# Encoder block, stage 1: V in 2 KB runs, stores issued by GpSimd, modulation sums spread over three projections

## The chip, the cores and the metric

The kernel runs on one core of one Trainium2 chip. The metric is the device time of one execution in microseconds (us), taken as the median of several runs.

## The reference

One encoder block over 1024 tokens of width 1024, all in float32, cut here to what stage 1 and its neighbours compute:

```python
mod = silu(c) @ w_ada + b_ada                 # six vectors of 1024
shift1, scale1, gate1, shift2, scale2, gate2 = split(mod, 6)
h = rms_norm(x, norm1_g) * (1 + scale1) + shift1
z = h @ w_in                                  # columns: c_q 256, c_kv 256, k_pe 64, dq 512, dk 512, dv 512
q  = rms_norm(c_q)  @ w_q_up                  # 4 heads x (128 + 64 rotary)
kv = rms_norm(c_kv) @ w_kv_up                 # 4 heads x (128 K + 128 V)
mla = softmax(q k^T) v                        # 4 heads
diff = (softmax(q1 k1^T) - lam * softmax(q2 k2^T)) dv   # 4 heads
x = x + gate1 * (concat[mla, diff] @ w_out)
h2 = rms_norm(x, norm2_g) * (1 + scale2) + shift2
x = x + gate2 * hier_moe(h2)                  # 32 experts
out = rms_norm(x, final_norm_g)
```

## The kernel before, in words

The kernel goes through stage 1 (all projections, to about 345 us of the span), the attention stage, the output projection with the router, and the experts. Every product in float32 precision is made of three passes (`mm3`, lines 67 to 69), from a high and a low part of each operand.

Stage 1 keeps the transposed, normalised activations (`hThi`, `hTlo`) in SBUF and walks over blocks of columns of `w_in`, and in each over 8 tiles of 128 tokens. A tile takes 24 matmuls (8 pieces of the width times three passes) into one PSUM buffer `pz` of four; DVE and ACT empty it. The blocks that matter here:

- The part called s1b makes dk. After four tiles come eight "flips": TensorE transposes four rotated tiles into a PSUM buffer `ptr` of two (line 180), ACT copies it to `stg` (line 409), DVE writes the low part `kl` (line 410), and both are stored to DRAM in `qk_d`. `stg` and `kl` share six buffers. The sixteen flips are woven into the following matmuls.
- The part s1c makes dv: `split_v` writes high and low part to `vs`, two buffers of one tile each, and stores each of the two with a DMA of 128 x 4 pieces of 512 bytes to `vd_d`.
- The part s1d makes c_q (g = 0) and c_kv with k_pe (g = 1). For each tile ACT sums the squares (line 472, output `junk`), ACT and DVE make the scale, DVE writes `cn`, and TensorE flips `cn`.
- The part s1e makes the MLA queries, keys and V from the latents: `split_v` again (to `vm_d`), and for heads 1 to 3 tiles `stg`, stored to `mq_d` by the helper `store`.

Beside this run the last four vectors of `mod` (gate1, shift2, scale2, gate2), which later stages read. `ada_in` loads 32 pieces `aw` of 512 KB of `w_ada`, three ahead; `ada_add` multiplies each by a column of silu(c) and adds it to `acc` (the first of eight on POOL, line 383, seven on DVE, line 385); the tables `AS` and `AC` say how many products belong to each tile of s1b and s1c. `ada_out` sums over the partitions with TensorE into a column of 128 x 8, adds the bias, and stores this column to `ada_d`, where the neighbours in memory lie on neighbouring partitions.

All loads and stores of stage 1 are issued by SP, in one order, each waiting for its data or its buffer. The order on the other engines is made by the scheduler of the kernel language from the program and its pools; what a pool's memory held before must be free before a new tile uses it. The attention stage begins with POOL scaling the exponentials `e` (lines 833, 776, 779), which TensorE then transposes.

```python
    def store(dst, src):
        Y.dma_start(f32(dst), f32(src))
...
                acc[v] = ap.tile([128, D], F32, name="acc", tag="acc")
                G.tensor_scalar(acc[v], w, sc[:, 0:1], 1.0, op0=ALU.mult, op1=ALU.mult)
...
        Y.dma_start(ada_d[0, (2 + v) * D:(3 + v) * D].rearrange("(j p) -> p j", p=128), col)
```

Of the kernel before, what the change touches and what calls it, by code (L numbers as in the profile page):

```python
# [9 lines left out]
F32 = mybir.dt.float32  # L10
F32R = mybir.dt.float32r
BF16 = mybir.dt.bfloat16
I32 = mybir.dt.int32
AF = mybir.ActivationFunctionType
ALU = mybir.AluOpType
# [5 lines left out]
D = 1024  # L21
# [10 lines left out]
LH = (3, 0)  # L32
XL = (0, 0, 0, 4)
WM = ((0, 1), (0, 1), (0, 0), (0, 0))
AS = (2, 2, 2, 2, 2, 2, 2, 2)
AC = (2, 2, 2, 2, 2, 2, 2, 2)
PF = 7
KJ, PL = 4, 6
GU1 = 10
# [10 lines left out]
def tile_hymba(  # L50
# [6 lines left out]
    V, A, G, T, Y = nc.vector, nc.scalar, nc.gpsimd, nc.tensor, nc.sync  # L57
    dbg = dbg or {}

    def f32(ap):  # L60
        return ap.bitcast(F32)
# [12 lines left out]
    ident = consts.tile([128, 128], F32, name="ident")  # L74
# [14 lines left out]
    ada_d = dram.tile([1, 6 * D], F32, name="ada_d")  # L89
# [27 lines left out]
    hTlo = hTp.tile([128, 8, S], F32R, name="hTlo")  # L117

    def store(dst, src):
        Y.dma_start(f32(dst), f32(src))  # L120

    def w_tiles():
        return (wp.tile([128, 4, 512], F32, name="wraw", tag="wraw", bufs=2),
# [62 lines left out]
        V.scalar_tensor_tensor(lo, src_lo, scale, f32(hi_lo), op0=ALU.mult, op1=ALU.subtract)  # L186

    def split_v(pool, pz, dst, t):
        vs = pool.tile([128, 2, 512], F32R, name="vs", tag="vs", bufs=2)
        A.copy(vs[:, 0], pz)  # L190
        V.tensor_sub(vs[:, 1], pz, f32(vs[:, 0]))
        for l in range(2):
            Y.dma_start(f32(dst[:, :, t, l].rearrange("h p d -> p h d")),
                        f32(vs[:, l].rearrange("p (h d) -> p h d", h=4)))

    def zps():
        return ps1.tile([128, 512], F32, name="pz", tag="z", bufs=4)
# [149 lines left out]


    aps = ExitStack()
    ap = aps.enter_context(tc.tile_pool(name="s1m", bufs=2, side="right", **RT))  # L350

    aw, acc = {}, {}

# [6 lines left out]
    def ada_out(v):  # L360

        pr = mps()
        for j in range(8):
            T.matmul(pr[:, j:j + 1], acc[v][:, j * 128:(j + 1) * 128], ones[:, 0:1], start=True, stop=True)
        col = ap.tile([128, 8], F32, name="col", tag="col")
        V.tensor_add(col, pr[:, 0:8], colsb[:, 16 + 8 * v:24 + 8 * v])
        Y.dma_start(ada_d[0, (2 + v) * D:(3 + v) * D].rearrange("(j p) -> p j", p=128), col)

    def ada_add(n):

        for _ in range(n):
            i = ada_at[0]
            ada_at[0] += 1
            if i == 0:
                for k in range(AB):
                    ada_in(k)
            v, k = divmod(i, 8)
            if k == KO and v:
                ada_out(v - 1)
            w = aw.pop(i)  # L380
            if k == 0:
                acc[v] = ap.tile([128, D], F32, name="acc", tag="acc")
                G.tensor_scalar(acc[v], w, sc[:, 0:1], 1.0, op0=ALU.mult, op1=ALU.mult)
            else:
                V.scalar_tensor_tensor(acc[v], w, sc[:, k:k + 1], acc[v], op0=ALU.mult, op1=ALU.add)
            ada_in(i + AB)
# [45 lines left out]
    with tc.tile_pool(name="s1c", bufs=2, **RT) as sb:  # L432
        w = in_w(1600, 512)
        for t in range(NT):
            if t == 4:
                in_w(0, 256)
            pz = zps()
            in_proj(t, 512, w, pz)
            split_v(sb, pz, vd_d, t)
            ada_add(AC[t])  # L440
        ada_out(3)
    aps.close()

    cTp = cTs.enter_context(tc.tile_pool(name="cT", bufs=1, side="right", **RT))
    cThi = cTp.tile([128, 4, S], F32R, name="cThi")
# [8 lines left out]
    with tc.tile_pool(name="s1d", bufs=2, **RT) as sb:  # L454
        for g in range(2):
            width = 320 if g else 256
            w = in_w(256 * g, width)
            for half in range(2):
                if half:
                    if g:  # L460
                        up_w = [load_up(w_q_up, 768), load_up(w_kv_up, 1024)]
                    else:
                        in_w(256, 320)
                cns, rps = [], []
                hs = slice(half * 512, half * 512 + 512)
                for t in range(4 * half, 4 * half + 4):
                    pz = zps()
                    in_proj(t, width, w, pz[:, :width])
                    cn = sb.tile([128, 256], F32, name="cn", tag="cn", bufs=6)
                    junk = sb.tile([128, 256], F32, name="junk2", tag="junk2", bufs=1)  # L470
                    st = sb.tile([128, 4], F32, name="st2", tag="st2", bufs=4)
                    A.activation(junk, pz[:, :256], AF.Square, accum_out=st[:, 0:1])
                    A.activation(st[:, 1:2], st[:, 0:1], AF.Sqrt, bias=epsc, scale=1.0 / 256)
                    V.reciprocal(st[:, 2:3], st[:, 1:2])
                    V.tensor_scalar(cn, pz[:, :256], st[:, 2:3], None, op0=ALU.mult)
                    cns.append(cn)
                    if g:
                        rp = sb.tile([128, 1, 2, 64], F32, name="rpk", tag="rpk", bufs=5)
                        rope(sb, pz[:, 256:320].rearrange("p (m h d) -> p m h d", m=1, h=2), 1, t, rp)
                        rps.append(rp)  # L480
                for j in range(2):
                    jj = 2 * g + j
                    ptr = flip([cn[:, j * 128:j * 128 + 128] for cn in cns])
                    gcol = colsb[:, 56 + jj:57 + jj]
                    A.activation(cThi[:, jj, hs], ptr, AF.Copy, scale=gcol)
                    V.scalar_tensor_tensor(cTlo[:, jj, hs], ptr, gcol, f32(cThi[:, jj, hs]),
                                           op0=ALU.mult, op1=ALU.subtract)
                if g:
                    ptr = flip([rp[:, 0].rearrange("p c d -> p (c d)") for rp in rps])
                    A.copy(K1pe[:, hs], ptr)  # L490
                    V.tensor_sub(KLpe[:, hs], ptr, f32(K1pe[:, hs]))
    qw, kw = up_w
    hTs.close()

# [28 lines left out]
    with tc.tile_pool(name="s1e", bufs=2, **RT) as sb:  # L523
        load_head("d", 0, 0)
        load_head("d", 0, 1)
        heads["m", 0] = [[tile_a() for _ in range(5)], None]

        def to_m(h, i, hs):

            if h == 0:  # L530
                return heads["m", 0][0][i][:, hs], lambda: None
            st = sb.tile([128, 512], F32R, name="stg", tag="stg", bufs=6)
            return st, lambda: store(mq_d[h, i, :, hs], st)

        qv = [w_.rearrange("p r (h e) -> p r h e", h=4)[:, :, :, 128:192] for w_ in qw]
        kv = [w_.rearrange("p r (h e) -> p r h e", h=4)[:, :, :, 128:256] for w_ in kw]
        for half in range(2):
            hs = slice(half * 512, half * 512 + 512)
            rps = []
            for t in range(4 * half, 4 * half + 4):  # L540
                ts = slice(t * 128, t * 128 + 128)
                pz = zps()
                for r in range(2):
                    mm3(pz[:, :256], cThi[:, r, ts], cTlo[:, r, ts], qv[0][:, r], qv[1][:, r], r == 0, r == 1)
                rp = sb.tile([128, 4, 2, 64], F32, name="rpq", tag="rpq", bufs=6)
                rope(sb, pz[:, :256].rearrange("p (m h d) -> p m h d", m=4, h=2), 4, t, rp)
                rps.append(rp)
                pz = zps()
                for r in range(2):
                    mm3(pz, cThi[:, 2 + r, ts], cTlo[:, 2 + r, ts], kv[0][:, r], kv[1][:, r], r == 0, r == 1)  # L550
                split_v(sb, pz, vm_d, t)
            for h in range(4):
                ptr = flip([rp[:, h].rearrange("p c d -> p (c d)") for rp in rps])
                st, put = to_m(h, 4, hs)
                split_q(st, st[64:128], ptr, ptr[64:128], st[64:128], MSC)
                put()
        for h in range(4):
            for src, (whi, wlo), base in ((0, qw, h * 192), (2, kw, h * 256)):
                for half in range(2):
                    hs = slice(half * 512, half * 512 + 512)  # L560
                    pz = zps()
                    for r in range(2):
                        mm3(pz, whi[:, r, base:base + 128], wlo[:, r, base:base + 128],
                            cThi[:, src + r, hs], cTlo[:, src + r, hs], r == 0, r == 1)
                    (sh, put_h), (sl, put_l) = to_m(h, src, hs), to_m(h, src + 1, hs)
                    if src == 0:
                        split_q(sh, sl, pz, pz, sh, MSC)
                    else:
                        A.copy(sh, pz)
                        V.tensor_sub(sl, pz, f32(sh))  # L570
                    put_h()
                    put_l()
# [981 lines left out]
```

## Time and profile before

| | |
|---|---|
| median of 3 runs | 1444.3 us (1442.43 to 1444.31) |
| the profiled execution, whole time | 1447.06 us |
| its span, first to last instruction | 1445.3 us |
| TensorE matmul busy | 1337.1 us (93%) |
| VectorE (DVE) busy | 993.9 us (69%) |
| ScalarE (ACT) busy | 681.8 us (47%) |
| GpSimd (POOL) busy | 416.9 us (29%) |
| moved by DMA | 361.22 MB, mean 250 GB/s |

Busy times are of one execution, and an engine's share is over the whole span. PE is TensorE's matmuls, PEld its weight loads; SPq is SP's queue of DMAs. "Idle before <- X" is the time an engine stood still before an instruction, and what ended it. The granted clock is the share of full speed that TensorE was given: 1.0 is its level of 2.4 GHz and 0.5 its level of 1.2 GHz, and a stretch with something between had both. The DMA share is the mean busy share of the 16 DMA engines.

### The profile page before, as it was taken

The page shows a single profiled execution, that of the slowest core. Times are in us where ns is not written, and L with a number is a line of the kernel's source. Part 1 is how long each engine was busy: PE and PEld are TensorE (multiplying, and loading weights), DVE is VectorE, ACT ScalarE, POOL GpSimd, SP SyncE. Part 2 cuts the span into 40 slices and gives each one's busy share as a digit, 9 for nine tenths or more (in the row PEclk, how much of TensorE's full clock was granted, in tenths as well). Part 3 has the DMA queues.
Part 4 walks back from the last instruction along what each step waited for, and adds up shares of the span by engine and source line. Part 5 has one row for each costly group of instructions (what it writes and reads, how often), then busy time and mean ns, then how long its engine had stood idle before and what let it go on. Part 6 is the DMA issues. An engine that isn't in the chain of part 4 may idle for free. (4 is left out here: it accounts for less than half of the span.)

```text
span 1445.3 us, 17733 instructions
## 1 busy us (share of the span) xinstructions
PE 1337.1 (93%) x6211; PEld 961.9 (67%) x6211; DVE 993.9 (69%) x1530; ACT 681.8 (47%) x1058; POOL 416.9 (29%) x285
## 2 busy tenths in 40 slices
PE   5799896998999999989995999999999998999993
PEld 4578676986788888878884655566565555656541
DVE  6888553475788888884568766676766668666646
ACT  4642212454766666661214554444554444544523
POOL 3100000002766666650002233333333322111231
PEclk9899898999999999999995999999999999999995
DMA  9537799268043433337968999999988998999956
GB/s 328 150 100 249 198 298 209 55 223 302 1 152 125 139 130 140 132 112 261 340 224 297 339 354 315 348 366 354 345 297 297 327 348 308 347 359 338 372 181 238
DMA packets 197502, 361.22 MB, mean 250 GB/s; under 512 B 20101, under 2 KB 62146, under 8 KB 195874
## 3 DMA queue, kind: packets, MB, share of 16 engines
q1 hardware_dynamic: 132946, 228.97, 47.2%
q10 hardware_dynamic: 57024, 113.25, 21.9%
q0 software_dynamic: 7440, 17.84, 5.2%
q8 instruction: 50, 0.82, 0.2%
q14 instruction: 42, 0.34, 0.1%
HBM read 306.52 MB, written 61.88 MB: 255 GB/s over the span
## 5 line engine op out<-in xcount | busy, mean ns | idle before, releaser
L1153 DVE TENSOR_TENSOR ra<-rb,ra 128x1024 fp32r<-128x1024 f32 x180 | 210.8, 1217 | 42.4 <-ACT ra L1152 42.2
L1152 ACT CAST ra<-rb 128x1024 fp32r<-128x1024 f32 x180 | 181.5, 1050 | 93.4 <-PE pg L69 34.2
L1319 POOL DMA_INDIRECT x_d<-y,tg x32 | 139.2, 4351 | 132.5 <-DVE y L1351 130.3
L1349 PE MATMUL pd<-rb,hmT 128*96 128x512 f32 x368 | 165.1, 592 | 0.0
L604 PE MATMUL s<-ra 128*128 128x512 f32 x448 | 129.5, 405 | 2.5 <-ACT e L625 2.4
L1351 DVE SCALAR_TENSOR_TENSOR y<-pd,wt,ra 96x512 f32<-96x512 f32 x64 | 47.8, 747 | 121.5 <-PE pd L1349 121.5
L67 PE MATMUL pz<-whi,hThi 128*128 128x512 f32 (+2 forms) x320 | 122.3, 382 | 9.6 <-ACT hThi L255 5.1
L625 ACT ACTIVATE e<-s,mx 128x1024 f32<-128x1024 f32 x96 | 107.6, 1120 | 38.5 <-DVE mx L620 21.8
L620 DVE TENSOR_REDUCE mx<-s 128x1 f32<-128x1024 f32 x96 | 116.6, 1217 | 12.2 <-PE s L604 12.2
L68 PE MATMUL pz<-wlo,hThi 128*128 128x512 f32 (+2 forms) x320 | 120.6, 377 | 1.5 <-DVE wlo L131 1.5
L930 POOL DMA_INDIRECT xb<-h_d,tg x31 | 31.5, 1017 | 313.4 <-PE ptr L1326 312.8
L69 PE MATMUL pz<-whi,hTlo 128*128 128x512 f32 (+2 forms) x320 | 116.0, 370 | 0.3 <-DVE hTlo L257 0.3
L67 PE MATMUL pg<-ra,xT 128*96 128x512 f32 x256 | 114.1, 446 | 0.2 <-ACT xT L1369 0.2
L1349 PEld LDWEIGHTS pd<-rb,hmT 128*96 128x96 f32 x368 | 58.2, 163 | 77.6 <-issue 74.5
L68 PE MATMUL pu<-ra,xT 128*96 128x512 f32 x256 | 102.6, 401 | 3.7 <-DVE ra L1153 3.7
L69 PE MATMUL pg<-ra,xT 128*96 128x512 f32 x256 | 102.1, 399 | 2.8 <-DVE xT L1370 2.8
L67 PE MATMUL pu<-ra,xT 128*96 128x512 f32 x256 | 103.7, 405 | 0.0
L1153 DVE TENSOR_TENSOR ra<-rx,ra 128x1024 fp32r<-128x1024 f32 x76 | 89.6, 1217 | 19.2 <-ACT ra L1152 19.2
L636 ACT CAST rb<-ptr 128x512 fp32r<-128x512 f32 x128 | 74.4, 588 | 59.8 <-PE ptr L632 59.2
L68 PE MATMUL pg<-ra,xT 128*96 128x512 f32 x256 | 102.0, 398 | 0.0
L69 PE MATMUL pu<-ra,xT 128*96 128x512 f32 x256 | 100.7, 393 | 0.0
L1152 ACT CAST ra<-rx 128x1024 fp32r<-128x1024 f32 x76 | 76.8, 1047 | 38.6 <-PE pg L69 11.5
(336 smaller groups left out, 2813.2 us busy)
## 6 DMA issues: line engine op xcount, KB each, us to landing
rb<-in_w_expert_up_dram ACTq DMA_DIRECT2D x26, 1024.0 KB, 16.7
rb<-in_w_expert_down_dram ACTq DMA_DIRECT2D x26, 1024.0 KB, 9.2
rb<-in_w_expert_gate_dram ACTq DMA_DIRECT2D x24, 1024.0 KB, 12.7
rb<-in_w_expert_gate_dram SPq DMA_DIRECT2D x20, 1024.0 KB, 15.6
rb<-in_w_expert_down_dram SPq DMA_DIRECT2D x20, 1024.0 KB, 9.2
rb<-in_w_expert_up_dram SPq DMA_DIRECT2D x19, 1024.0 KB, 10.3
aw<-in_w_ada_dram SPq DMA_DIRECT2D x32, 512.0 KB, 5.0
ra<-qk_d SPq DMA_DIRECT2D x24, 512.0 KB, 6.0
```

Source lines behind the costliest of these rows:

```text
L67: T.matmul(ps, ahi, bhi, start=first, stop=False)
L68: T.matmul(ps, ahi, blo, start=False, stop=False)
L69: T.matmul(ps, alo, bhi, start=False, stop=last)
L604: T.matmul(ps[:, ns], l, r[:, ns], start=i == 0, stop=i == len(parts) - 1)
L620: V.reduce_max(mx, ps, axis=AX.X, negate=True)
L625: A.activation(e, ps, AF.Exp, bias=nb, scale=1.0, accum_out=z)
L636: A.copy(hi[:, :, q], src)
L1152: A.copy(hi, raw[:, 2 * half:2 * half + 2])
L1153: V.tensor_sub(lo, raw[:, 2 * half:2 * half + 2], f32(hi))
L1319: G.indirect_dma_start(out=x2_d, out_offset=bass.IndirectOffsetOnAxis(ap=si, axis=0), in_=y, in_offset=None, bounds_check=S - 1, oob_is_er ...
L1349: T.matmul(pd, hT[:, k], w[:, k], start=k == 0, stop=k == 3)
L1351: V.scalar_tensor_tensor(y[:, ns], pd, wcol, gate2[:, ns], op0=ALU.mult, op1=ALU.mult)
```

## The change

- `store` issues on POOL's queue in place of SP's; this takes in the stores of `qk_d`, `mq_d` and both V.
- `split_v` gathers two token tiles in a `vs` of twice the size and stores them with one DMA of 128 x 4 pieces of 2 KB, in place of four DMAs of 128 x 4 pieces of 512 bytes.
- The modulation products go one to a tile (`AS`, `AC`, and a new `AG` for s1d) in place of two; their pool moves to the left side of SBUF and closes after s1d.
- The first product of each vector is made by ACT in place of POOL.
- `ada_out` transposes its column to 8 rows of 128, ACT copies them, and POOL's queue stores 8 runs of 512 bytes.
- In s1e `stg` and `rpq` have five buffers in place of six.

```diff
-AS = (2, 2, 2, 2, 2, 2, 2, 2)
-AC = (2, 2, 2, 2, 2, 2, 2, 2)
+AS = (1, 1, 1, 1, 1, 1, 1, 1)
+AC = (1, 1, 1, 1, 1, 1, 1, 1)
+AG = ((1, 1, 1, 1, 1, 1, 1, 1), (1, 1, 1, 1, 1, 1, 1, 1))
     def store(dst, src):
-        Y.dma_start(f32(dst), f32(src))
+        G.dma_start(f32(dst), f32(src))
     def split_v(pool, pz, dst, t):
-        vs = pool.tile([128, 2, 512], F32R, name="vs", tag="vs", bufs=2)
-        A.copy(vs[:, 0], pz)
-        V.tensor_sub(vs[:, 1], pz, f32(vs[:, 0]))
-        for l in range(2):
-            Y.dma_start(f32(dst[:, :, t, l].rearrange("h p d -> p h d")),
-                        f32(vs[:, l].rearrange("p (h d) -> p h d", h=4)))
+        if t % 2 == 0:
+            vpair.append(pool.tile([128, 4, 2, 2, 128], F32R, name="vs", tag="vs", bufs=2))
+        hi, lo = (vpair[-1][:, :, t % 2, l] for l in range(2))
+        pv4 = pz.rearrange("p (h d) -> p h d", h=4)
+        A.copy(hi, pv4)
+        V.tensor_sub(lo, pv4, f32(hi))
+        if t % 2:
+            store(dst[:, :, t - 1:t + 1].rearrange("h p t l d -> p h (t l d)"),
+                  vpair[-1].rearrange("p h t l d -> p h (t l d)"))
-    ap = aps.enter_context(tc.tile_pool(name="s1m", bufs=2, side="right", **RT))
+    ap = aps.enter_context(tc.tile_pool(name="s1m", bufs=2, **RT))
-        Y.dma_start(ada_d[0, (2 + v) * D:(3 + v) * D].rearrange("(j p) -> p j", p=128), col)
+        T.transpose(pr[0:8, 128:256], col, ident)
+        row8 = ap.tile([8, 128], F32, name="row8", tag="row8")
+        A.copy(row8, pr[0:8, 128:256])
+        G.dma_start(ada_d[0, (2 + v) * D:(3 + v) * D].rearrange("(j p) -> j p", p=128), row8)
-                G.tensor_scalar(acc[v], w, sc[:, 0:1], 1.0, op0=ALU.mult, op1=ALU.mult)
+                A.activation(acc[v], w, AF.Copy, scale=sc[:, 0:1])
...
+                    ada_add(AG[g][t])
+                if g == 1 and half:
+                    ada_out(3)
-            st = sb.tile([128, 512], F32R, name="stg", tag="stg", bufs=6)
+            st = sb.tile([128, 512], F32R, name="stg", tag="stg", bufs=5)
-                rp = sb.tile([128, 4, 2, 64], F32, name="rpq", tag="rpq", bufs=6)
+                rp = sb.tile([128, 4, 2, 64], F32, name="rpq", tag="rpq", bufs=5)
```

The order of SP's queue from the end of s1c into s1d, before (`wraw` are pieces of `w_in` and of the two up-projections):

```order
L358 DMA aw<-in_w_ada_dram 128x1024 x2
L193 DMA vd_d<-vs 128x4x128 x2
L358 DMA aw<-in_w_ada_dram 128x1024
L367 DMA ada_d<-col 128x8x1
L193 DMA vd_d<-vs 128x4x128 x2
L129 DMA wraw<-in_w_in_dram 128x4x320
L367 DMA ada_d<-col 128x8x1
L129 DMA wraw<-in_w_in_dram 128x4x320
L449 DMA wraw<-in_w_q_up_dram 128x2x768
L449 DMA wraw<-in_w_kv_up_dram 128x2x1024
```

And SP's whole queue from s1b to the end of s1d in the change (line 358 of before is 365 here, 129 is 131, 449 is 457):

```order
L131 DMA wraw<-in_w_in_dram 128x4x256
L365 DMA aw<-in_w_ada_dram 128x1024 x13
L131 DMA wraw<-in_w_in_dram 128x4x256
L365 DMA aw<-in_w_ada_dram 128x1024 x2
L131 DMA wraw<-in_w_in_dram 128x4x320
L365 DMA aw<-in_w_ada_dram 128x1024 x10
L131 DMA wraw<-in_w_in_dram 128x4x320
L365 DMA aw<-in_w_ada_dram 128x1024 x2
L457 DMA wraw<-in_w_q_up_dram 128x2x768
L365 DMA aw<-in_w_ada_dram 128x1024 x4
L457 DMA wraw<-in_w_kv_up_dram 128x2x1024
```

The stores have left SP's queue, and four `aw` loads now stand ahead of the keys' up-projection.

POOL's order around the end of stage 1, before:

```order
L383 TENSOR_SCALAR acc<-aw,sc 128x1024 x4
L833 TENSOR_SCALAR e<-e,zd 128x1024
L776 TENSOR_SCALAR e<-e,zd 128x1024
L779 TENSOR_TENSOR e<-e 128x512 x2
```

And in the change, from the V of s1c on (lines 833 and 776 of before are 845 and 788):

```order
L122 DMA vd_d<-vs 128x4x512 x3
L377 DMA ada_d<-row_1634 8x128
L122 DMA vd_d<-vs 128x4x512
L377 DMA ada_d<-row_1957 8x128
L122 DMA vm_d<-vs 128x4x512 x2
L122 DMA mq_d<-stg 128x512 x3
L122 DMA vm_d<-vs 128x4x512 x2
L122 DMA mq_d<-stg 128x512 x27
L845 TENSOR_SCALAR e<-e,zd 128x1024
L788 TENSOR_SCALAR e<-e,zd 128x1024
```

Twenty-seven stores in a row stand on POOL ahead of its first instruction of the attention stage.

## Rows read from the trace of the kernel before

**Rows 1.** Busy time by stretch, s1b to s1e; the first line names the columns.

```profile
core 0: us, PE busy (x) PEld busy (x) DVE busy (x) ACT busy (x) POOL busy (x), PEclk, DMA share, GB/s
138.00:345.00 207.00, 184.64 (x1025) 160.22 (x1023) 115.50 (x214) 68.68 (x144) 3.37 (x3) 0.93 0.76 211
```

**Rows 2.** Timeline of PE, 138 to 262 us: instructions after a long idle time.

```profile
148.89 0.65 PE L180 MATMUL ptr<-ident,rp 128*128 128x128 f32 x4 [2.03 <-DVE kl L410]
...
178.44 1.11 PE L180 MATMUL ptr<-ident,rp 128*128 128x128 f32 x4 [4.91 <-DVE kl L410]
...
183.29 1.11 PE L180 MATMUL ptr<-ident,rp 128*128 128x128 f32 x4 [1.18 <-DVE kl L410]
...
229.18 0.58 PE L67 MATMUL pz<-whi,hThi 128*128 128x256 f32 x1 [4.10 <-ACT whi L130]
231.29 0.58 PE L68 MATMUL pz<-wlo,hThi 128*128 128x256 f32 x1 [1.53 <-DVE wlo L131]
...
250.71 0.66 PE L180 MATMUL ptr<-ident,cn 128*128 128x128 f32 x2 [5.81 <-DVE cn L475]
```

**Rows 3.** Busy time by stretch, ahead of, around and behind these idle times.

```profile
120.00:140.00 20.00, 20.00 (x91) 16.17 (x90) 16.37 (x25) 2.69 (x5) 1.13 (x1) 1.00 0.83 269
...
148.00:160.00 12.00, 11.11 (x49) 9.71 (x50) 6.89 (x12) 4.56 (x7) 0.00 (x0) 0.72 0.52 195
...
172.00:176.00 4.00, 1.53 (x7) 0.91 (x5) 0.00 (x0) 0.20 (x1) 0.00 (x0) 1.00 0.78 37
176.00:188.00 12.00, 8.39 (x27) 6.58 (x28) 5.81 (x7) 0.59 (x1) 1.12 (x1) 0.57 0.86 256
...
228.00:236.00 8.00, 5.29 (x26) 5.00 (x27) 6.85 (x7) 1.71 (x3) 0.00 (x0) 0.57 1.02 350
...
248.00:256.00 8.00, 5.29 (x28) 5.32 (x28) 3.55 (x9) 4.84 (x14) 0.00 (x0) 0.57 1.05 95
```

**Rows 4.** Timeline of ACT, 140 to 262 us: three instructions that waited for a store.

```profile
147.50 0.59 ACT L409 CAST stg<-ptr 128x512 fp32r<-128x512 f32 x1 [4.07 <-DMA qk_d<-stg]
...
222.98 0.59 ACT L190 CAST vs<-pz 128x512 fp32r<-128x512 f32 x1 [10.10 <-DMA vd_d<-vs]
...
247.76 0.38 ACT L472 ACTIVATE junk<-pz 128x256 f32<-128x256 f32 x1 [15.29 <-DMA vd_d<-vs]
```

**Rows 5.** Timeline of DVE: a product that waited for its load.

```profile
176.49 1.28 DVE L385 SCALAR_TENSOR_TENSOR acc<-aw,sc,acc 128x1024 f32<-128x1024 f32 x1 [5.24 <-DMA aw<-in_w_ada_dram]
```

**Rows 6.** DMA issues, 60 to 400 us: the column's stores, KB each, median us to landing.

```profile
ada_d<-col SPq DMA_DIRECT2D x4, 4.0 KB, 13.1
```

**Rows 7.** Packets of all DMA in the stretch 168 to 180 us.

```profile
DMA packets 1418, 1.07 MB, mean 89 GB/s; under 512 B 1070, under 2 KB 1187, under 8 KB 1418
```

**Rows 8.** Packets of all DMA in 303 to 313 us, V of s1e.

```profile
DMA packets 3442, 2.66 MB, mean 266 GB/s; under 512 B 134, under 2 KB 3177, under 8 KB 3441
```

**Rows 9.** Groups of POOL's instructions over the whole span: busy us, mean ns of one.

```profile
L1319 POOL DMA_INDIRECT x_d<-y,tg x32 | 139.2, 4351 | 132.5 <-DVE y L1351 130.3 <-DVE rb L1444 2.2
...
L930 POOL DMA_INDIRECT xb<-h_d,tg x31 | 31.5, 1017 | 313.4 <-PE ptr L1326 312.8 <-issue 0.3 <-POOL xb L927 0.3
...
L1136 POOL DMA_DIRECT2D rb<-in_w_expert_up_dram x1 | 0.9, 867 | 0.0
```

**Rows 10.** Timeline of ACT, end of stage 1: first and last of twelve copies.

```profile
328.19 0.60 ACT L185 ACTIVATE stg<-pz 128x512 fp32r<-128x512 f32 x1 [0.77 <-PE pz L69]
...
343.15 0.59 ACT L569 CAST stg<-pz 128x512 fp32r<-128x512 f32 x1 [0.77 <-PE pz L69]
```

**Rows 11.** Timeline of SP's queue, end of stage 1.

```profile
324.69 20.11 SPq L120 DMA_DIRECT2D mq_d<-stg  x27
```

**Rows 12.** Timeline of POOL: its first instruction of the attention stage.

```profile
347.14 1.13 POOL L833 TENSOR_SCALAR e<-e,zd 128x1024 f32<-128x1024 f32 x1 [124.84 <-DVE zd L832]
```

**Rows 13.** The tile stg, 100 to 360 us: its stores, issue to landing.

```profile
DMA to landing us min/median/max: 2.0/2.7/5.2
```

**Rows 14.** Busy time by stretch, the body of s1d.

```profile
260.00:280.00 20.00, 20.00 (x147) 19.74 (x147) 10.02 (x28) 8.49 (x25) 0.00 (x0) 1.00 0.16 54
```

More of the change, by code (lines that the diff above doesn't have):

```diff
@@ L188, in split_v @@
     def split_v(pool, pz, dst, t):
-        vs = pool.tile([128, 2, 512], F32R, name="vs", tag="vs", bufs=2)
-        A.copy(vs[:, 0], pz)
-        V.tensor_sub(vs[:, 1], pz, f32(vs[:, 0]))
-        for l in range(2):
-            Y.dma_start(f32(dst[:, :, t, l].rearrange("h p d -> p h d")),
-                        f32(vs[:, l].rearrange("p (h d) -> p h d", h=4)))
+        if t % 2 == 0:
[7 more added lines that the diff above has]
+                  vpair[-1].rearrange("p h t l d -> p h (t l d)"))
+    vpair = []
     def zps():
@@ L440, in tile_hymba @@
             ada_add(AC[t])
-        ada_out(3)
-    aps.close()
     cTp = cTs.enter_context(tc.tile_pool(name="cT", bufs=1, side="right", **RT))
@@ L491, in tile_hymba @@
                     V.tensor_sub(KLpe[:, hs], ptr, f32(K1pe[:, hs]))
+    aps.close()
     qw, kw = up_w
```

## The prediction

> **What bounds the kernel now.** I first read the busy times by stretch. TensorE is the busiest engine, and in the 207 us that the change touches it stands still for 207.00 - 184.64 = 22.4 us, at a mean clock of 0.93 [rows 1]. So the question is which of its idle times the change takes away, and what comes in their place.
>
> The timeline of PE then names six long idle times [rows 2]: 2.03 at 148.9, 4.91 and 1.18 before 184, 4.10 and 1.53 before 231.3, 5.81 before 250.7; together 19.6 us. Behind each the granted clock falls to a mix of its two levels (1.2 and 2.4 GHz) [rows 3]. I count the loss as busy time times one minus clock: 11.11 x 0.28 = 3.1 us in 148 to 160, 8.39 x 0.43 = 3.6 in 176 to 188, 5.29 x 0.43 = 2.3 each in 228 to 236 and 248 to 256. Idle plus clock is 5.1 us at the first place and 25.7 us at the three others (17.5 idle, 8.2 clock). These are 30.8 us at stake.
>
> PE's rows name DVE or ACT, so I went on to what these waited for. At 176.5 DVE waited 5.24 us for a load `aw` [rows 5], with flips' low parts `kl` queued behind it. At 223.0 ACT waited 10.10 us and at 247.8 it waited 15.29 us for stores of V, and at 147.5 it waited 4.07 us for a store of `stg` [rows 4]; behind it stood the weight cast and the squares that PE needed. So DMA ends last in every case.
>
> Why is DMA late? In 172 to 176 us the engines are 0.78 busy and move 37 GB/s, in 248 to 256 they are 1.05 busy and move 95 GB/s [rows 3]. In 168 to 180, 1070 of 1418 packets are under 512 bytes [rows 7]. That is the column store of `ada_out`: 128 x 8 single floats, 4 KB in 1024 packets, with a median of 13.1 us to landing, four times [rows 6]. V's 512-byte pieces alone run at 266 GB/s [rows 8], so they are not the slow ones.
>
> **The change part by part.** *Modulation store and V runs.* Each column store goes from 1024 packets to 8 runs of 512 bytes, and V's pieces from 512 bytes to 2 KB, a quarter of the count. What waits for them are the three places worth 25.7 us. At best all of it goes. At the other end the largest place (5.81 + 2.3 = 8.1) stays, because the first flip of s1d hangs on a chain through ACT and DVE anyway: 17.6. I take half of that idle time as staying, 2.9: **-22.8**. Late next is then the weight cast at the border of s1c and s1d.
>
> *Stores of dk on POOL.* SP's queue no longer holds stores behind `aw` loads that wait for a buffer, and the reverse. At best the 5.1 us of the first place go. Against it, a flip's two stores cost POOL 2 x 0.867 = 1.7 us by its only direct transfer [rows 9], while six of the eight flips of a half stand close together in PE's order, some five matmuls apart: these take 20 / 91 = 0.22 us each [rows 3], a flip's own four transposes 0.65 [rows 2], of which a part overlaps, so a flip can come every 1.5 us. POOL needs 6 x 1.73 = 10.4 us where PE takes 9, 1.4 more, in two halves about 3 us of new waiting. Ends -5.1 and +3; I take **-2**, as `stg` and `kl` have six buffers and the first three flips need no wait.
>
> *Stores of the MLA tiles on POOL, the tail.* Twelve copies of `stg` start at 328.19 to 343.15, so one pair of stores every 14.96 / 11 = 1.36 us, 0.68 a store [rows 10]; SP kept up with that, its 27 stores in 20.11 us following the data [rows 11]. POOL at 0.867 does not: 24 x (0.867 - 0.68) = 4.5 us behind at the end. Its first `e` starts at 347.14 [rows 12]; with the last data at 343.15 + 0.6 + 0.7 = 344.5 and one store, POOL would have been free at 345.3, so 1.8 us are slack: 2.7 us late, and PE waits there. With five buffers and a landing some 0.55 us later than SP's 2.7 [rows 13], a pair needs (0.05 + 3.25) / 2 = 1.65 us, no more than the 1.73 of two issues. Below: a store has 128 pieces where the 867 ns transfer has 512, so perhaps no loss, 0. Above: the gather's 1.017 [rows 9], 24 x 0.337 - 1.8 = 6.3. I take the nearest row, 0.867, rounded up: **+3**. The scatter's 4.35 us on the same engine belongs to a rival.
>
> The rows speak against this one move: POOL is dearer than the pace, and SP was not late here. The Trainium skill says so too ("DMA: Bandwidth & Descriptors", section "Issuing engine by pattern"): plain stores belong on SP, GpSimd is for indirect transfers. By that rule the sum would be 3 us better with these stores left on SP; the rows agree for the tail.
>
> *First products on ACT.* Four of about 1.2 us, twice the 0.6 of a copy of half the size [rows 10], go from POOL to ACT, which is busy 68.7 of 207 us [rows 1]. That cover makes it nothing; if `aw` came late, ACT would stand with what is queued behind, as in rows 4, some 4 us.
>
> *Products moved to s1d.* Eight of 1.28 us [rows 5] come to 10.2 us of DVE over some 50 us in which it is busy 10.02 of 20, and 4 MB where DMA is busy 0.16 of the time [rows 14]: nothing. Four `aw` loads now stand ahead of the keys' up-projection on SP's queue; they wait for DVE's products, each 1.28 us, so it costs nothing unless DVE is behind.
>
> *Four transposes, four small copies.* At most 0.33 us of PE each by the 0.66 of two at the low clock [rows 2], 1.3; I take **+0.8**. *Five buffers for `rpq`*: between nothing and one pace of 1.36; I take **+0.5**.
>
> Sum: -22.8 - 2 + 3 + 0.8 + 0.5 = **-20.5 us**. The profiled execution took 1447.06, which gives 1426.6. The median of the runs shown, 1444.3, is 2.8 us lower, and the same sum from there gives 1423.8: I forecast **1424**. With all best ends, -25.7 - 5.1 = -30.8, it is 1413.5; with all worst, -17.6 + 3 + 6.3 + 1.3 + 1.4 = -5.6, it is 1438.7.
>
> **The rivals.** *POOL becomes the brake in s1b.* The stores of a flip hold `stg` and `kl`, ACT and DVE wait, PE idles and its clock falls again. For it: 1.7 us a flip against flips 1.5 us apart. Against it: over a half POOL has 16 x 0.867 = 13.9 us of work, while PE has 4 x 24 matmuls of 0.22 and eight flips of some 0.65, 26 us. Price: +3 instead of -2, 3.1 us of clock, and the tail at its worst, +3.3: 1424 + 11.4 = 1435.
>
> *Bytes, not packets, are the limit.* Around 228 to 236 the engines move 350 GB/s at a share of 1.02 [rows 3]; there no packet count helps, and only the 4 MB moved out do. Then 4.10 + 1.53 + 2.3 = 7.9 us stay, and s1b gains nothing, 2 more: 1434. Against it: 37 and 95 GB/s at the two other places. The Trainium skill ("DMA: Bandwidth & Descriptors", "Issuing engines are not separate DMA queues") holds that transfers from SP and POOL share the same 16 engines, so that a second issuer saves only issue time; by that rule the move to POOL frees no bandwidth. The DMA shares near 1 agree; no run before has stores on POOL.
>
> *Both of these*: the two prices together, 11.4 + 9.9, give 1424 + 21.3 = 1445, no change.
>
> *Slower: POOL's issue is far dearer than 0.87.* The scatter takes 4.35 us [rows 9]. The break-even is where the tail eats the other 23.5 us: 24 x (c - 0.68) - 1.8 = 23.5, c = 1.73. At half the scatter, 2.2, the tail costs 34.7 and each half of s1b 16 x 2.2 = 35 us on POOL against 26 on PE, 18 more: 1444.3 - 23.5 + 34.7 + 18 = 1473.5. Against it: the only direct transfer, with four times the pieces, took 0.867.
>
> **How the numbers follow.** Forecast 0.62, POOL in s1b 0.16, bytes 0.10, both 0.06, POOL far dearer 0.06. Faster by over 0.2% (2.9 us, about what a measurement of this kernel tells from no change) are the first three: 0.88. Of the 0.06 for both, 0.05 is within 0.2%, and 0.01 goes with the 0.06 of slower: 0.07. The range reaches from 1413 to 1439, the ends of the forecast, and takes in the rivals at 1435 and 1434; the other two cases, 0.12, lie outside, with the forecast's own margins.
>
> **What would show it.** Right: `ada_d` lands in a few us and no stretch before 260 has a DMA share near 1 with under 150 GB/s; ACT's waits for V of 10 and 15 us are gone; PE idles under 6 us between 138 us and the end of s1d, at a clock of 0.97 or more; DVE in s1d is some 10 us busier; POOL's store takes 0.7 to 1.0 us, and its first `e` comes 2 to 3 us late against the last copy. Wrong: PE waits again for `kl` or `whi` with ACT or DVE waiting for a store on POOL's queue; stores over 1.7 us each; or gaps of PE in s1d on `cn` because DVE waits for `aw`.

## The result and the profile after

The change takes 1433.26 us, the median of 4 runs (1430.06 to 1434.81); the kernel before takes 1443.78 beside it. The ratio is 0.9926 [0.9907, 0.9944], a gain of 10.5 us. The forecast was 1424, a gain of 20.5. The profiled execution took 1430.06, its span 1428.3, 17.0 less than before's 1445.3. Before's profiled execution, 1447.06, is slower than all the runs of its median, and the change's is its fastest, so differences between these two traces come out some 6 us larger than the gain of the medians.

The same stretches as in [rows 1] and [rows 3] first, and then s1e, in the change. The columns are us, then busy time of PE, PEld, DVE, ACT and POOL, then PE's clock, DMA share and GB/s.

```profile
138.00:345.00 207.00, 187.90 (x1071) 160.73 (x1070) 124.21 (x227) 80.52 (x165) 52.24 (x83) 0.97 0.65 234
...
172.00:176.00 4.00, 2.62 (x11) 2.16 (x12) 1.88 (x2) 1.17 (x2) 1.96 (x4) 0.73 1.03 421
248.00:256.00 8.00, 7.86 (x56) 7.59 (x56) 5.20 (x20) 2.80 (x10) 0.00 (x0) 1.00 0.00 1
281.00:330.00 49.00, 41.67 (x204) 32.52 (x202) 30.92 (x63) 22.17 (x42) 19.31 (x34) 0.97 0.86 322
```

The mean clock over 138 to 345 is 0.97 where it was 0.93, and 248 to 256 us, where the DMA engines were full at 95 GB/s, is a stretch in which they rest (the work is some 20 us further on by then; the start of s1d, 210 to 220 us in the change, has a share of 0.90 at 279 GB/s). At 172 us the share is 1.03 and was 0.78, but at 421 GB/s in place of 37: the place is full of bytes now, no more of packets.

PE's idle times, to be held against [rows 2]:

```profile
155.57 0.65 PE L182 MATMUL ptr<-ident,rp 128*128 128x128 f32 x4 [1.50 <-ACT rp L177]
...
172.05 0.66 PE L182 MATMUL ptr<-ident,rp 128*128 128x128 f32 x4 [2.90 <-DVE kl L420]
174.26 1.12 PE L182 MATMUL ptr<-ident,rp 128*128 128x128 f32 x4 [1.33 <-DVE kl L420]
...
293.23 0.50 PE L68 MATMUL pz<-whi,cThi 128*128 128x512 f32 x1 [1.63 <-DVE vs L196]
...
326.05 2.60 PE L616 MATMUL s<-ra 128*128 128x512 f32 x8 [3.20 <-DVE stg L582]
330.01 2.07 PE L616 MATMUL s<-ra 128*128 128x512 f32 x4 [1.35 <-ACT e L637]
334.23 1.12 PE L644 MATMUL ptr<-ident,e 128*128 128x128 f32 x4 [2.15 <-POOL e L791]
```

The waits at the two borders of s1c and s1d, 4.10 + 1.53 and 5.81 us, are gone. The waits for `kl` in s1b stay, 4.2 us where they were 6.1 (of the 2.03 at 148.9, 1.50 stand at 155.6, now for a rotated tile). New are waits in s1e and a longer one at its end.

The modulation store lands in half the time ([rows 6] had 13.1 us); dk's stores land in twice theirs, though before's trace holds the landing of only four of them. The last line is before's:

```profile
qk_d<-stg POOLq DMA_DIRECT2D x16, 256.0 KB, 5.8
...
ada_d<-row POOLq DMA_DIRECT2D x4, 4.0 KB, 6.2
...
qk_d<-stg SPq DMA_DIRECT2D x16, 256.0 KB, 2.6
```

The timeline of ACT, one copy of s1b and four of the end of stage 1, where [rows 10] had a copy every 1.36 us:

```profile
169.48 0.58 ACT L419 CAST stg<-ptr 128x512 fp32r<-128x512 f32 x1 [3.59 <-DMA qk_d<-stg]
...
306.86 0.60 ACT L187 ACTIVATE stg<-pz 128x512 fp32r<-128x512 f32 x1 [0.82 <-PE pz L70]
308.17 0.60 ACT L187 ACTIVATE stg<-pz 128x512 fp32r<-128x512 f32 x1 [0.71 <-PE pz L70]
311.74 0.59 ACT L581 CAST stg<-pz 128x512 fp32r<-128x512 f32 x1 [2.97 <-DMA mq_d<-stg]
...
326.25 0.58 ACT L581 CAST stg<-pz 128x512 fp32r<-128x512 f32 x1 [1.38 <-DMA mq_d<-stg]
```

ACT waits for stores again: for dk's in s1b, and at the end for those of the MLA tiles. Twelve copies take 19.39 us from first to last, where they took 14.96. The 4.43 more are one stall, 311.74 - 308.17 - 1.36 = 2.2 us, and a slower pace after it, nine steps in 14.51, 1.61 each, 2.3 us. PE meanwhile fills the four `pz` (it is busy 6.00 us from 306 to 312) and then waits with ACT: 1.26 us from 318 to 324, and the 3.20 before 326.05.

POOL's own part, by the view of the tile `stg` from 300 us (ns min/median/max) and POOL's timeline ([rows 12] had 347.14):

```profile
L122 POOL DMA_DIRECT2D mq_d<-stg x27: 540/540/552, 303.5 to 327.9; - x27
```

```profile
330.26 1.12 POOL L845 TENSOR_SCALAR e<-e,zd 128x1024 f32<-128x1024 f32 x1 [1.83 <-DVE zd L844]
```

A store costs POOL 0.54 us, not 0.867, and it is POOL that waits for data (27 x 0.54 = 14.6 us of the 24.9 from the first issue to the end of the last). SP's queue, freed of its stores, has meanwhile gone on to the loads of the attention stage; the second one falls into the stretch of the stall:

```profile
275.26 0.32 SPq L528 DMA_DIRECT2D vt<-vd_d  x1
...
304.54 0.32 SPq L528 DMA_DIRECT2D vt<-vm_d  x1
```

The MLA stores issued from 305.0 to 309.1 us land in 4.4 to 6.1 us, those after 312 us in 2.4 to 3.3.

So the balance is this. The first tile `rpq` of s1e is written at 304.3 us before and at 280.6 in the change: 23.7 us won. From there to the first exponential on ACT it takes 41.3 us before and 48.1 now: 6.8 lost again. The rows are before's two and then the change's two:

```profile
L174 DVE TENSOR_TENSOR rpq<-rt,rt x8: 411/414/426, 304.3 to 319.6; 128x256 f32<-128x256 f32 x8
345.65 1.11 ACT L625 ACTIVATE e<-s,mx 128x1024 f32<-128x1024 f32 x1 [0.61 <-DVE mx L620]
...
L176 DVE TENSOR_TENSOR rpq<-rt,rt x8: 410/413/426, 280.6 to 299.4; 128x256 f32<-128x256 f32 x8
328.75 1.11 ACT L637 ACTIVATE e<-s,mx 128x1024 f32<-128x1024 f32 x1 [0.62 <-DVE mx L632]
```

### The profile page after: what moved, and what is told of

Its sections match the earlier page's. It is cut to its first block, busy times and chain, and to the rows that moved or that the text cites. A ratio compares the mean times of both kernels' runs of the same rounds, so it can differ in the third digit from the quotient of the medians.

```text
span 1428.3 us, 17727 instructions
## 1 busy us (share of the span) xinstructions
PE 1331.1 (93%) x6215; PEld 955.4 (67%) x6215; DVE 992.1 (69%) x1530; ACT 687.1 (48%) x1066; POOL 467.5 (33%) x371
## 3 DMA queue, kind: packets, MB, share of 16 engines
q0 software_dynamic: 15984, 46.70, 10.5%
## 5 line engine op out<-in xcount | busy, mean ns | idle before, releaser
L1331 POOL DMA_INDIRECT x_d<-y,tg x32 | 144.3, 4509 | 129.7 <-DVE y L1363 127.1
L69 PE MATMUL pz<-wlo,hThi 128*128 128x512 f32 (+2 forms) x320 | 117.3, 366 | 0.3 <-DVE wlo L133 0.3
L616 PEld LDWEIGHTS s<-ra 128*128 128x128 f32 x448 | 81.6, 191 | 23.0 <-ACT e L637 4.3
```

Source lines behind the costliest of these rows:

```text
L69: T.matmul(ps, ahi, blo, start=False, stop=False)
L616: T.matmul(ps[:, ns], l, r[:, ns], start=i == 0, stop=i == len(parts) - 1)
L1331: G.indirect_dma_start(out=x2_d, out_offset=bass.IndirectOffsetOnAxis(ap=si, axis=0), in_=y, in_offset=None, bounds_check=S - 1, oob_is_er ...
```

## The experiments

Beside the kernel before, whose median was 1446 to 1447 us in these comparisons, the ratios were:

| run | what it is | us | ratio to before |
|---|---|---|---|
| e1 | before, row store alone | 1430.1 | 0.9891 [0.9876, 0.9907] |
| e3 | change, column store back | 1463.4 | 1.0116 [1.0101, 1.0132] |
| e4 | the change again | 1432.8 | 0.9908 [0.9893, 0.9924] |
| e2 | change, MLA stores on SP | 1424.8 | 0.9851 [0.9838, 0.9865] |
| e6 | change, products two to a tile | 1444.6 | 0.9984 [0.9968, 1.0000] |
| e7 | change, V in 512 bytes | 1440.6 | 0.9958 [0.9941, 0.9975] |
| e8 | e7 with six buffers | 1438.7 | 0.9948 [0.9931, 0.9965] |
| e9 | change, the last MLA store on SP | 1430.1 | 0.9878 [0.9850, 0.9906] |
| e10 | change, dq, dk and MLA stores on SP | 1418.0 | 0.9807 [0.9790, 0.9824] |
| e5 | change, all stores on SP | 1417.0 | 0.9803 [0.9787, 0.9819] |
| e11 | e5, products two to a tile | 1423.7 | 0.9843 [0.9824, 0.9863] |
| e12 | e5, V in 512 bytes | 1421.3 | 0.9818 [0.9798, 0.9838] |

Differences of two ratios are turned into us below with 1445 (0.001 is 1.4 us). An interval is 0.003 to 0.006 wide, so such a difference is known to some 3 us.

**e1: the row store alone, in the kernel before.**

```diff
-        Y.dma_start(ada_d[...].rearrange("(j p) -> p j", p=128), col)
+        T.transpose(pr[0:8, 128:256], col, ident)
+        row8 = ap.tile([8, 128], F32, name="row8", tag="row8")
+        A.copy(row8, pr[0:8, 128:256])
+        Y.dma_start(ada_d[...].rearrange("(j p) -> j p", p=128), row8)
```

> The kernel before, with one part of the change: the modulation column is transposed, copied by ACT and stored as 8 runs of 512 bytes, on SP's queue as before. Theory 'packets' (the 1024-packet column stores hold the DMA engines, and the three large stalls of PE come from that): 12 to 20 us below the kernel before, about 1424 to 1432 us, ACT's waits of 10 and 15 us for V's stores shrink below 5, no stretch between 160 and 260 with a DMA share near 1 under 150 GB/s. Theory 'bytes' (the modulation loads and V's stores together are too much for these stretches): within 5 us of the kernel before.

Measured: 16 us faster, at least as much as the whole change (1432.8 beside it, e4; the intervals overlap), with V still in 512-byte pieces and every store on SP. 138 to 345 us in its trace:

```profile
138.00:345.00 207.00, 194.54 (x1092) 166.05 (x1091) 129.65 (x237) 80.26 (x167) 15.84 (x14) 0.96 0.68 234
```

PE is busy 9.9 us more in the stretch than in [rows 1]. In place of the idle times of [rows 2] PE has 1.51 us for `kl`, 1.38 for `col` and 0.73 for `cn`. Of ACT's waits of 10.10 and 15.29 us for V the first is 5.46, a little over what was expected, and the second is gone. The four stores of 1024 packets were what made the DMA late.

**e3: the column store back, in the change.**

```diff
-        T.transpose(pr[0:8, 128:256], col, ident)
...
-        G.dma_start(ada_d[...].rearrange("(j p) -> j p", p=128), row8)
+        Y.dma_start(ada_d[...].rearrange("(j p) -> p j", p=128), col)
```

> The changed kernel with the column store of 1024 packets back, on SP's queue; all else as changed. Theory 'packets': the stalls come back, 8 to 20 us above the changed kernel, near the kernel before. Theory 'bytes': within 3 us of the changed kernel, since products are spread and V goes in 2 KB runs.

Measured: 30 us slower than the change, 17 slower than before. The store's landing in its DMA issues, and PE's longest idle times:

```profile
ada_d<-col SPq DMA_DIRECT2D x4, 4.0 KB, 12.9
```

```profile
224.87 0.58 PE L69 MATMUL pz<-wlo,hThi 128*128 128x256 f32 x1 [10.09 <-DVE wlo L133]
...
263.08 0.64 PE L69 MATMUL pz<-wlo,hThi 128*128 128x320 f32 x1 [8.95 <-DVE wlo L133]
```

With the column store, the other parts of the change together cost time. Row store and column store are two sides of 16 us in the kernel before, and of 30 in the change.

**e4: the change again**, on the chip of e1 to e3.

> The changed kernel once more, for the size and spread of its gain. If the first profiled execution (17 us below in span) is typical, the ratio is near 0.989; if the median of the first runs is, near 0.9925, and another execution shows where the missing 5 us lie: in the MLA tail if its pace varies (1.36 to 2 us a pair), in the flips of dk if PE's idle time between 138 and 185 us varies.

Measured: 0.9908 beside the first 0.9926; the same idle times (3.22 us at 172.5, 3.44 at 327.2), and 48.1 us again from the first `rpq` (281.8) to the first exponential (329.92).

**e2: the MLA stores back on SP.**

```diff
-            return st, lambda: store(mq_d[h, i, :, hs], st)
+            return st, lambda: Y.dma_start(f32(mq_d[h, i, :, hs]), f32(st))
```

> The changed kernel, but the 30 stores of the MLA tiles (mq_d) go back to SP's queue. Theory 'POOL's issue makes the tail slow': the twelve copies of stg come every 1.36 us again in place of 1.76, 4 to 5 us below the changed kernel. Theory 'five buffers and a landing slowed by the loads that now run beside the stores': the pace stays above 1.6 us and the gain is under 2 us.

Measured: 0.0057 below the change beside it, 8 us. First and last of the twelve copies:

```profile
307.76 0.60 ACT L187 ACTIVATE stg<-pz 128x512 fp32r<-128x512 f32 x1 [0.82 <-PE pz L70]
...
322.75 0.59 ACT L581 CAST stg<-pz 128x512 fp32r<-128x512 f32 x1 [0.77 <-PE pz L70]
```

14.99 us for eleven steps, 1.36 each, with the same five buffers: five do, when SP issues. From the first `rpq` (284.1) to the first exponential (325.35) it is 41.3 us as before. Two causes were left, since SP's queue also changes its order: the stores now stand ahead of the attention stage's loads.

**e9, e8 and e7: the loads that ran ahead, the buffers, and V's runs.** e9 puts the last of the thirty MLA stores on SP, so that the load of `vm_d` waits behind it:

```diff
+            if h == 3 and i == 3 and hs.start == 512:
+                return st, lambda: Y.dma_start(f32(mq_d[h, i, :, hs]), f32(st))
             return st, lambda: store(mq_d[h, i, :, hs], st)
```

> The change with the very last of the thirty MLA stores on SP's queue, so that SP's load of vm_d and two loads of qk_d, 2 MB, wait behind it until the end of stage 1; the other 29 stores stay on POOL, with five buffers. Theory 'collision': the loads had taken the bandwidth; the copies come every 1.36 to 1.45 us, the time is 1425 to 1428. Theory 'buffers': the copies stay at 1.6 us or more each, the time is 1431 to 1435. If both hold, the stall of 3 us at 311 goes and a pace of 1.6 stays: 1429 to 1431.

e7 takes V back to four stores of 512-byte pieces for two tiles, and e8 uses the memory that this frees for six buffers of `stg` and `rpq`:

```diff
-        if t % 2 == 0:
-            vpair.append(pool.tile([128, 4, 2, 2, 128], F32R, name="vs", tag="vs", bufs=2))
...
+        vs = pool.tile([128, 2, 512], F32R, name="vs", tag="vs", bufs=2)
...
+        for l in range(2):
+            store(dst[:, :, t, l].rearrange("h p d -> p h d"),
+                  vs[:, l].rearrange("p (h d) -> p h d", h=4))
```

> The change with V stored per token tile in pieces of 512 bytes again (four stores for two tiles, two small vs buffers), still issued by POOL. Theory 1: the 2 KB runs are worth 3 us or more, since packets of 512 bytes fill the DMA engines in s1c and s1e: 1436 to 1440, with ACT waiting for stores of V. Theory 2: they are worth nothing, or cost a little, because a pair holds its buffer until both tiles are written and 1 MB has landed (7.6 us in the change): 1431 to 1434, and PE's two idle times at 293 and 295 us, 2.3 us together, shrink below 1.

> The kernel before this one in the list (V in small pieces), with six buffers for stg and rpq in place of five; the MLA stores are still issued by POOL. Theory 'buffers' (a store issued by POOL holds its buffer longer, so five are too few): the last twelve copies of stg come every 1.36 to 1.45 us and not every 1.76, and the time is 4 to 8 us below that of the run with small pieces and five buffers. Theory 'collision' (with its stores gone, SP's queue loads 1 MB of the attention stage's V at 304 us, into a stretch in which the stores alone need 380 GB/s): the copies stay at 1.6 us or more, and the time within 2.5 us of that run.

ACT's copies at the end of stage 1 in e9, five buffers and no load beside them:

```profile
306.13 0.60 ACT L187 ACTIVATE stg<-pz 128x512 fp32r<-128x512 f32 x1 [0.82 <-PE pz L70]
...
323.33 0.59 ACT L583 CAST stg<-pz 128x512 fp32r<-128x512 f32 x1 [1.10 <-DMA mq_d<-stg]
```

And in e8, six buffers and the load of `vm_d` issued at 312.27:

```profile
315.54 0.60 ACT L187 ACTIVATE stg<-pz 128x512 fp32r<-128x512 f32 x1 [0.76 <-PE pz L70]
319.07 0.59 ACT L578 CAST stg<-pz 128x512 fp32r<-128x512 f32 x1 [2.94 <-DMA mq_d<-stg]
...
331.62 0.59 ACT L578 CAST stg<-pz 128x512 fp32r<-128x512 f32 x1 [0.86 <-DVE stg L579]
```

Both theories hold, each for its half. In e9 the stall is gone and a pace of 17.20 / 11 = 1.56 stays; in e8 the stall of 3.53 stays and the pace after it is 12.55 / 9 = 1.39, where e7 with five buffers has 1.58. e9's median is where "if both hold" had put it. In time, from the first `rpq` to the first exponential: 48.1 us in the change and in e4, 43.3 in e9, 41.3 in e2. So the loads cost 4.8 us, and five buffers under POOL's issue 2.0. The ratios say 4 to 7 and 4, within their noise. e8's time fell by only 2 us against e7, which is inside the noise and less than the theory of buffers had said.

e7 itself cost 0.003 to 0.005 against the change, 5 to 7 us. PE and ACT in e7:

```profile
292.49 0.69 PE L182 MATMUL ptr<-ident,rpq 128*128 128x128 f32 x2 [5.91 <-ACT rpq L177]
```

```profile
291.55 0.58 ACT L192 CAST vs<-pz 128x512 fp32r<-128x512 f32 x1 [7.25 <-DMA vm_d<-vs]
```

At that point SP has already issued nine loads of `qk_d` and one of `vd_d` for the attention stage (272 to 278 us), and from 280 to 290 us the DMA share is 1.02. e12 below, with V on SP, tells whether it was those loads.

**e6: the products two to a tile again.**

```diff
-AS = (1, 1, 1, 1, 1, 1, 1, 1)
-AC = (1, 1, 1, 1, 1, 1, 1, 1)
+AS = (2, 2, 2, 2, 2, 2, 2, 2)
+AC = (2, 2, 2, 2, 2, 2, 2, 2)
...
-                    ada_add(AG[g][t])
-                if g == 1 and half:
-                    ada_out(3)
```

> The change with the modulation products two to a tile again, in s1b and s1c alone, as before; everything else as in the change. Theory 1: spreading them takes 4 MB of loads out of s1c and is worth 4 to 8 us, as the rival 'bytes, not packets' held: PE idles at the border of s1c and s1d again for 4 us or more (the weight cast late), and the time is 1437 to 1441. Theory 2: once the column store is gone, the DMA engines carry these loads beside V (the kernel of before with the row store alone idled 0.7 us there): no gain from spreading, 1433 within 2.5 us, and s1d has 10 us less of DVE work.

Measured: no gain over before is left, 0.006 to 0.008 more than the change, 8 to 11 us; past both theories, and not at the border of s1c and s1d but in s1b. ACT and PE there:

```profile
181.51 0.59 ACT L419 CAST stg<-ptr 128x512 fp32r<-128x512 f32 x1 [5.82 <-DMA qk_d<-stg]
```

```profile
183.37 1.11 PE L182 MATMUL ptr<-ident,rp 128*128 128x128 f32 x4 [4.44 <-DVE kl L420]
```

PE idles only little more in s1b than in the change (7.0 us in waits of over 1 us, for 5.7), but behind the waits its granted clock is lower: 0.86 from 138 to 200 us, for 0.97. With PE 55.0 and 56.1 us busy there, busy time times one minus clock is 7.7 us for 1.7. Just before these flips, from 165.6 to 173.9 us, SP had issued five `aw` loads and a piece of `w_in`; the `kl` stores of 175.0 to 177.0 us landed in 8.9 to 10.2 us, and in the change none took over 8.5. e1 has the same products, but its stores on SP, and idles there for 1.5 us. This led to the next run.

**e10: dk's stores on SP as well** (V and the row stay on POOL). The edit also takes back the sixteen stores of dq, ahead of s1b (tile `s`, 98 to 122 us); PE idles in neither run there.

```diff
-                    store(qk_d[h, 2 + i, :, hs], st)
-                    store(qk_d[h, 4 + i, :, hs], kl)
+                    Y.dma_start(f32(qk_d[h, 2 + i, :, hs]), f32(st))
+                    Y.dma_start(f32(qk_d[h, 4 + i, :, hs]), f32(kl))
```

> The change with the stores of dk and of the MLA tiles on SP's queue again; V's stores and the modulation row stay on POOL. Beside the run with the MLA stores alone on SP (ratio 0.985 to before). Theory 'one queue keeps loads behind stores': on SP the aw loads stand behind dk's stores and leave them the DMA engines (in the kernel of before with the row store, no aw load is issued from 142 to 161 us), on POOL both run at once and a dk store lands in 5 to 6 us in place of 2.7; so PE's idle times in s1b, 5.7 us of one microsecond or more in the change, shrink below 2.5, and the ratio is 0.981 to 0.983. Theory 'bytes': the same 13 MB cross s1b either way and PE waits as before: the ratio is 0.984 to 0.987. Rival: the aw loads and the weights wait behind stores on SP, DVE falls behind in s1c and s1d, and the ratio is 0.988 or more.

Measured: 0.0044 below e2, 6.4 us, just below the 0.981 to 0.983 that the theory of one queue had named. The stretch of dk's stores in the change, by busy times, and the landing of `qk_d` from 100 to 185 us (min/median/max; dq's stores are among them):

```profile
138.00:180.00 42.00, 36.05 (x176) 28.91 (x176) 31.92 (x42) 15.45 (x24) 16.54 (x31) 0.96 0.95 333
```

```profile
DMA to landing us min/median/max: 2.3/5.2/8.5
```

The same two views of e10:

```profile
138.00:180.00 42.00, 42.00 (x211) 34.39 (x211) 30.83 (x42) 16.58 (x25) 1.01 (x1) 1.00 0.96 335
```

```profile
DMA to landing us min/median/max: 2.0/3.0/4.5
```

Share and bandwidth are the same, 333 and 335 GB/s; what differs is whose bytes go first. Of dk's stores alone, the change's trace holds 28 landings with a median of 5.6 us, and e10's only four, 3.0 to 4.5. A rival that no theory named is that POOL's issue itself makes a store land late. dq's stores in the change speak against it: on POOL too, those of 108 to 117 us land in 2.3 to 2.5 us (2.0 in the one landing that e10 shows), and those issued from 117.3 us on in 4.0 to 6.7. The first `aw` load goes out at 117.88. SP's queue in e10 shows the order that does it:

```profile
147.89 0.83 SPq L421 DMA_DIRECT2D qk_d<-stg  x1
148.81 0.38 SPq L422 DMA_DIRECT2D qk_d<-kl  x1
149.25 7.45 SPq L365 DMA_DIRECT2D aw<-in_w_ada_dram  x4
```

From 137 to 149 us the queue holds stores alone, and the `aw` loads, which nobody needs yet, stand behind them. PE does not idle in these 42 us.

**e5, e11, e12: everything on SP**; then with the products of e6, or with V as in e7.

```diff
     def store(dst, src):
-        G.dma_start(f32(dst), f32(src))
+        Y.dma_start(f32(dst), f32(src))
...
-        G.dma_start(ada_d[...].rearrange("(j p) -> j p", p=128), row8)
+        Y.dma_start(ada_d[...].rearrange("(j p) -> j p", p=128), row8)
```

> The change with every store, V's pairs and the modulation row too, on SP's queue; spread products, 2 KB runs and five buffers stay. Theory: with 2 KB runs V's four stores in s1c hold nobody up wherever they are issued: within 0.002 of the ratio of the run with dk and MLA stores on SP. Rival: on SP a 1 MB store stands between aw loads and the pieces of w_in, the weight cast at the border of s1c and s1d comes late, PE idles 2 to 4 us there: 0.003 worse or more.

> All stores on SP as in the run above, and the modulation products two to a tile in s1b and s1c alone, as before; so against the kernel of before with the row store alone (ratio 0.989) it has V in 2 KB runs, the first products on ACT and five buffers. Theory 'spreading pays only where stores and loads have two queues': the ratio is within 0.003 of the run above. Theory 'spreading pays anyway, since it takes 4 MB out of s1c': 0.004 to 0.008 above it, PE idling 2 us or more at the border of s1c and s1d.

> All stores on SP and the products spread, as in the run with ratio 0.980, but V stored per token tile in pieces of 512 bytes, in two buffers of half the size. Theory 1: 2 KB runs pay wherever V is issued (with V on POOL, the small pieces cost 7 us against the change): ACT waits for stores of vd_d or vm_d by 5 us or more, the ratio is 0.984 to 0.988. Theory 2: the small pieces hurt only where SP's queue ran ahead with the attention stage's loads beside them: on one queue the ratio is 0.979 to 0.982.

Measured: e5 is as fast as e10, so V's stores and the row may be issued by either. Its time is the lowest here, 28.5 us under before and 15 to 18 under the change. Spreading the products is worth 0.0040, 6 us, on one queue too, just where the second theory begins; in e11 PE waits for dk and at the border of s1c and s1d, where e5 has one wait of 0.95 us, and ACT waits for V in s1c, with the loads on the engines beside it:

```profile
148.80 0.66 PE L182 MATMUL ptr<-ident,rp 128*128 128x128 f32 x4 [1.79 <-DVE kl L420]
...
212.48 0.38 PE L374 MATMUL pmi<-ident,col 128*8 128x128 f32 x1 [2.95 <-DVE col L373]
```

```profile
197.01 0.59 ACT L195 CAST vs<-pz 128x512 fp32r<-128x512 f32 x1 [9.17 <-DMA vd_d<-vs]
```

The 2 KB runs are worth 0.0015, 2 us, with overlapping intervals: on one queue they matter little. There the loads of `vd_d` and three of `qk_d` wait behind the stores until 316 us, and where e7 idled for 5.91 us, PE's longest wait beside V in e12 is 0.40:

```profile
286.56 0.50 PE L68 MATMUL pz<-whi,cThi 128*128 128x512 f32 x1 [0.40 <-DVE vs L193]
```

## Why the prediction was right and wrong

The direction was right, and the time fell inside the range, but the gain was half of the forecast. The terms, measured as differences of ratios:

| term | forecast | measured |
|---|---|---|
| row store, 2 KB runs, small edits (before to e11) | -22.8 + 0.8 + 0.5 | -22.7 |
| products moved to s1d (e11 to e5) | 0 | -5.8 |
| V and row on POOL (e5 to e10) | not a term of its own | +0.6, within the noise |
| dk's stores (and dq's) on POOL (e10 to e2) | -2 | +6.4 |
| MLA stores on POOL (e2 to the change) | +3 | +8 to +11 |

*The modulation store and V's runs* held. The reading that packets and not bytes filled the engines [rows 3, 6, 7] is shown by e1 and e3, and the size came out within 2 us. Inside it the row store is 16 us by itself, and the remaining 7 of e11 are V's runs, the first products on ACT and the buffers together, not taken apart; the +0.8 and +0.5 were not measured by themselves.

*Products moved to s1d: nothing* was wrong by 6 us. I asked only whether s1d had room for them, which it had (DVE is 15.16 us busy from 240 to 260 and PE 19.86), and not what their leaving does for s1b and s1c, where DMA and ACT were late. My count was wrong too: `AG` gives s1d sixteen products, 8 MB, and not eight and 4 MB. In the trace eight of them run at 201 to 217 us, around the start of s1d at 212, and eight at 233 to 251. The rival of bytes had named that gain, but counted it as all that would be left.

*Stores of dk on POOL: -2* failed at the step "SP's queue no longer holds stores behind `aw` loads, and the reverse". The reverse is a service: loads held behind stores leave them the engines. I then compared POOL's 10.4 us of issuing with PE's 9, which was never the limit: POOL issued in 0.54 us and was busy 16.54 us of 42. The landing rose to 5.6 us from the 3.0 to 4.5 of e10, and the six buffers of `stg` and `kl` came free late. What happened looks like the rival "POOL becomes the brake in s1b", priced at 1435, and shows the sign that I had written under "Wrong": ACT waits for a store on POOL's queue and PE for `kl`. Its cause was another. The Trainium skill ("DMA: Bandwidth & Descriptors", section "Issuing engines are not separate DMA queues") says that DMAs from SP and GpSimd run on the same 16 engines and interleave there. The 333 and 335 GB/s agree; what e10 adds is that the interleaving itself has a price when one of the two is a prefetch.

*The tail: +3* was mis-sized by 5 to 8 us by the ratios, and by 4 in the traces of the change and of e4 (6.8 lost in each). The issue time was too high (0.867 for 0.54), and the two steps behind it were wrong the other way. The pace was set by five buffers at 1.56 to 1.61, which I had worked out as 1.65 and dropped as "no more than the 1.73 of two issues". And the slack of 1.8 us before the first `e` could not be used: the waits do not pile up behind POOL, they go back to ACT, whose copies take 4.4 us longer themselves, and through it to PE, and `e` follows 4.0 us after the last copy as it did before (330.26 - 326.25, and 347.14 - 343.15). Not seen at all was what SP does when its stores are gone, although the loads that stand next in its queue can be read from its order: 1 MB of the next stage came into a stretch where the stores alone need 256 KB in 0.68 us, 385 GB/s (e9). The Trainium skill's rule that plain stores belong on SP ("DMA: Bandwidth & Descriptors", section "Issuing engine by pattern"), which I set beside the sum for the tail alone, held for dk too: e10 took 1418.0 us.

Up to the start of s1e the sum was 24.0 us (22.8 + 2 - 0.8) and the trace gave 23.7 (22.5, 21.8 and 20.2 in e4, e9 and e2, whose code is the same up to there): nearly right, but by luck, since two errors cancel, 6 us of spread products unseen and some 8 us in s1b with the wrong sign.

Still open: why the row store is worth 30 us in the change and 16 before. That loads run further ahead of everything on two queues would explain it, but this was not tried apart. Nor has any run the stores on a second queue other than POOL's.

## What to carry to other kernels

A DMA queue's order is also a priority: stores that buffers wait for are held up less when the prefetches behind them sit on the same queue, so before moving stores to another engine, read what that queue would start in their place, and whose buffers come free late if it does. A transfer of a few KB with 4-byte elements counts by its packets; look for one wherever the DMA share is near 1 at a low rate. Where a ring of buffers sets the pace, time its whole hold (copy, issue, landing), and do not set the loss against a slack further down the line.

## What the runs showed of the hardware

POOL took 0.54 us to issue a store of 256 KB, 0.76 for one of 1 MB in 2 KB pieces, and SP 0.32 for the 256 KB (before). With two queues the 16 engines moved no more in s1b (333 GB/s with stores on POOL, 335 on SP), and a store of dk, 256 KB, landed in 5.6 us (median of 28) in place of 3.0 to 4.5 (four). Stores of the same size from POOL landed in 2.3 to 2.5 us just before the first `aw` load of that trace and in 4.0 to 6.7 beside it. The same 4 KB landed in 12.9 us as 1024 packets from SP (e3) and in 6.2 as 8 runs from POOL (the change).
